# Feed-forward of a two-layer trunk: the gated products turned by transposing transfers on 16-bit planes in place of TensorE transposes

## The chip, the core and the metric

One core of one Trainium2 chip runs one launch of the kernel. The metric is the device time of a launch in microseconds. A core has these engines, each with an instruction stream of its own that it works through in order: TensorE (PE in the profile: matmuls and transposes, with PEld for its weight loads), VectorE (DVE), ScalarE (ACT), GpSimd (POOL) and SyncE (SP), which here only issues transfers. SBUF is the memory on the chip, PSUM the place where TensorE writes its results, and 16 DMA engines move data between the chip's main memory and SBUF or inside SBUF.

## What is computed

A residual stream `h` of 256 tokens and 1024 features goes through two layers. Each layer is a feed-forward, a token mixer and another feed-forward; the mixer is a gated recurrence in the first layer and attention in the second. So there are four feed-forwards, and the change touches nothing else:

```python
def swiglu(x, w_gate, w_up, w_down):
    return (jax.nn.silu(x @ w_gate) * (x @ w_up)) @ w_down

f = swiglu(rms_norm(h, ffn1_pre_g[layer]), ffn1_w_gate[layer], ffn1_w_up[layer], ffn1_w_down[layer])
h = h + 0.5 * rms_norm(f, ffn1_post_g[layer])
```

`w_gate` and `w_up` have 1024 x 2816 elements, `w_down` 2816 x 1024. All data are 32-bit floats.

## The kernel before

**Tiles.** The 256 tokens are two tiles of 128, called t = 0 and t = 1. A matrix product is made to 32-bit accuracy from three matmuls on operands that are split into an upper part (rounded, name ending in hi) and a lower part (what is left, ending in lo): `mm3`, lines 181 to 185, whose three matmuls are lines 183, 184 and 185.

**Weights.** A weight unit is 128 x 1024 elements, 512 KB. `load_raw` (lines 156 to 165) has SP issue its transfer into one of `RAW` = 5 buffers `raw`; `split` (lines 167 to 179) makes the upper part `whi` on ACT (line 173) and the lower part `wlo` on DVE (line 177), each in a ring of `WB` = 9 buffers.

**Order of the work.** `items` is a list of pairs of a preparation (load and split of a unit) and a piece of work for one t. `run` (lines 376 to 389) sets the order on PE by hand: t = 0 goes ahead of t = 1 by `lag` units, which starts at `LAG` = 7 (3 in the first feed-forward), falls to `MID` = 4 within a few units and stays there until the last units. One call of `slot` (lines 367 to 374) is the work of one t on one unit, in a feed-forward 6 matmuls of 512 columns; it ends with a `tick` (lines 84 to 96). `defer(n, f)` has `f` called n + 1 ticks later, counting the tick that ends the same slot. Instructions of PE stay in the order in which they are written; on the other engines a scheduler may move them, and their order is fixed when the program is built.

**A feed-forward** (`ffn_items`, lines 484 to 555) has 44 units of gate and up and 22 of down: five times four units of gate and four of up, 512 columns wide, then four units with gate and up side by side, 256 columns each (`pair_items`). After a gate block, line 498 makes `sil` (ACT). After an up block, `post_up` (lines 502 to 531) multiplies into `prod` (line 510, DVE, 128 tokens x 512 columns). The down product needs these with the columns on the partitions, so they have to be turned. Line 515 has SP copy `prod` into `prr`, a buffer that is typed for TensorE's fast transposes; with `HT` = 5 ticks in between, `hidden_T` (lines 522 to 530) makes four 128 x 128 transposes on PE (line 525; two for the narrow block), for the 512-wide blocks of both t one behind the other, so eight. ACT (line 529) makes the upper part `hhi` from PSUM, DVE (line 530) the lower part `hlo`. A feed-forward has 12 such blocks, six of each t; the whole kernel has 40 wide ones and 8 narrow ones, 176 transposes.

**Buffers around the change.** `prod` has two buffers. The wide `prr` takes the tag `t1` of `hpool` (two buffers, used by the norm steps at the ends of a feed-forward too), the narrow one the tag `sil` (two buffers).

**GpSimd** does little: small steps of the norms (lines 198 and 200), zeroing of gate weights and issue of some small transfers in the first feed-forward, and bias rows of the attention (lines 948 to 975) in the third.

Of the kernel before, what the change touches and what calls it, by code (L numbers as in the profile page):

```python
# [9 lines left out]
F32 = mybir.dt.float32  # L10
F32R = mybir.dt.float32r
BF16 = mybir.dt.bfloat16
AF = mybir.ActivationFunctionType
ALU = mybir.AluOpType
AX = mybir.AxisListType

P = 128
# [9 lines left out]
EPS = 1e-6  # L27
RAW = 5
WB = 9
HT = 5  # L30
LAG = 7
MID = 4
NEG = -1e30
# [10 lines left out]
def trunk_kernel(ctx: ExitStack, tc: tile.TileContext, A: dict, out: bass.AP):  # L44
    nc = tc.nc
# [5 lines left out]
    hpool = ctx.enter_context(tc.tile_pool(name="h", bufs=1))  # L51
# [6 lines left out]
    def nm(s):  # L58
        uid[0] += 1
        return f"{s}_{uid[0]}"  # L60
# [7 lines left out]
    def trbank():  # L68
        return psum.tile([P, 512], F32, tag="tr", name=nm("tr"), bufs=2)
# [11 lines left out]
    def defer(n, fn):  # L81
        pend.append([n, fn])
# [23 lines left out]
    h = [hpool.tile([P, D], F32, tag=f"h{t}", name=f"h{t}") for t in range(2)]  # L106
# [9 lines left out]
    identr = cpool.tile([P, P], F32R, name="identr")  # L116
# [3 lines left out]
    warm = cpool.tile([P, 1], F32, name="warm")  # L120
    nc.scalar.activation(warm, mhalf, AF.Silu)

    def keep_busy(n):

        ps = trbank()
        for _ in range(n):
            nc.tensor.matmul(ps, nc.const_aps.tensor(1.0, (P, P), BF16), nc.const_aps.tensor(1.0, (P, 512), BF16),
                             start=True, stop=True)
# [38 lines left out]
    def split(rawv, parts, n, pieces=1, pin=False):  # L167
# [4 lines left out]
        for c in range(0, n, m):  # L172
            up = nc.scalar.activation(hi[:parts, c:c + m], rawv[:, c:c + m], AF.Copy)  # L173
            if settled[0] or pin:
# [28 lines left out]
    def square_sum(src, acc, f=1.0):  # L203
        junk = spool.tile([P, D], BF16, tag="junk", name=nm("junk"), bufs=1)
        nc.scalar.activation(junk[:, :src.shape[1]], src, AF.Square, scale=f, accum_out=acc)  # L205

# [10 lines left out]
    def x_upper(tp, dest, n):  # L217
# [4 lines left out]
        nc.vector.tensor_tensor(xg, tp.rearrange("p (a b) -> p a b", a=4), g, ALU.mult)  # L222
        nc.scalar.activation(xh[:, 4 * n:4 * n + 4, :], xg, AF.Copy)
        return xg
# [12 lines left out]
    def to_x_tiles(tps, dest):  # L237
# [3 lines left out]
        def operands(k):  # L241
            return tps[k // 4][:, k % 4 * P:(k % 4 + 1) * P], gT[:, gi + k:gi + k + 1]
        with tc.high_priority():
            for k in range(8):
                src, g = operands(k)
                nc.scalar.activation(xh[:, k, :], src, AF.Copy, scale=g)
            for k in range(8):
# [81 lines left out]
    def gain_bcast(src):  # L329
        gb = hpool.tile([P, D], F32, tag="gb", name=nm("gb"), bufs=1)  # L330
        nc.sync.dma_start(gb, src.partition_broadcast(P))
        return gb
# [58 lines left out]
    def proj_items(w, c0, nn, get_x, post, nk=8):  # L391

        kper = min(1024 // nn, 4)
        acc = {}

        for k0 in range(0, nk, kper):
            kn = min(kper, nk - k0)

            def fetch(k0=k0, kn=kn, pieces=1):
                return load_raw(w[k0 * P:(k0 + kn) * P, c0:c0 + nn].rearrange("(k p) n -> p k n", p=P), P, kn * nn, pieces)  # L400

            def prep(fetch=fetch, kn=kn):
                return split(fetch(), P, kn * nn)

            def work(t, u, k0=k0, kn=kn, i=len(items)):
                if i < OPEN:
                    if k0 + kn == nk:
                        post(t, first_acc[t][:, :nn])
                    return
                if k0 == 0:  # L410
                    acc[t] = mmbank()
                ps = acc[t][:, :nn]
                for j in range(kn):
                    k = k0 + j
                    mm3(ps, *get_x(t, k), u.hi[:, j * nn:(j + 1) * nn], u.lo[:, j * nn:(j + 1) * nn], k == 0, k == nk - 1)
                if k0 + kn == nk:
                    post(t, acc[t][:, :nn])
            if len(items) < OPEN:
                first_loads.append(fetch)
            items.append((prep, work))  # L420

    def pair_items(wa, wb, c0, nn, get_x, post):

        acc = {}

        for k0 in range(0, 8, 2):
            def prep(k0=k0):
                raw = new_raw()
                v = raw.rearrange("p (k s n) -> p k s n", k=2, s=2)
                for s, w in enumerate((wa, wb)):  # L430
                    nc.sync.dma_start(v[:, :, s, :], w[k0 * P:(k0 + 2) * P, c0:c0 + nn].rearrange("(k p) n -> p k n", p=P))
                return split(raw, P, 1024)

            def work(t, u, k0=k0):
                if k0 == 0:
                    acc[t] = mmbank()
                for j in range(2):
                    k = k0 + j
                    mm3(acc[t], *get_x(t, k), u.hi[:, j * 512:(j + 1) * 512], u.lo[:, j * 512:(j + 1) * 512], k == 0, k == 7)
                if k0 == 6:  # L440
                    post(t, acc[t][:, :nn], acc[t][:, nn:2 * nn])
            items.append((prep, work))
# [41 lines left out]
    def ffn_items(pool_of, wg, wu, wd, post_g, next_dests, last=False, normed=False):  # L484
        hid = {}
        sil = {}
        box = {}

        def hid_tiles(t):
            if t not in hid:  # L490
                hid[t] = (pool_of().tile([P, 22, P], F32R, tag=f"hhi{t}", name=nm("hhi"), bufs=1),
                          pool_of().tile([P, 22, P], F32R, tag=f"hlo{t}", name=nm("hlo"), bufs=1))
            return hid[t]

        def post_gate(c0, nn):
            def f(t, ps):
                s = pool_of().tile([P, 512], F32, tag="sil", name=nm("sil"), bufs=2)
                nc.scalar.activation(s[:, :nn], ps, AF.Silu, scale=rs[t][:, 0:1])  # L498
                sil[t] = s
            return f  # L500

        def post_up(c0, nn):
            alone = nn < 512
            made = []

            def f(t, ps):
                hh, hl = hid_tiles(t)
                s = sil[t][:, :nn]
                pr = pool_of().tile([P, 512], F32, tag="prod", name=nm("prod"), bufs=2)
                nc.vector.scalar_tensor_tensor(pr[:, :nn], ps, rs[t][:, 0:1], s, ALU.mult, ALU.mult)  # L510
                if alone:
                    moved = pool_of().tile([P, 512], F32R, tag="sil", name=nm("prr"), bufs=2)
                else:
                    moved = hpool.tile([P, 512], F32R, tag="t1", name=nm("prr"), bufs=2)
                nc.sync.dma_start(moved[:, :nn].bitcast(F32), pr[:, :nn])
                made.append((moved, hh, hl))
                if alone or t == 1:
                    todo = list(made)
                    made.clear()
                    defer(HT, lambda: [hidden_T(*m) for m in todo])  # L520

            def hidden_T(moved, hh, hl):
                tp = trbank()
                for j in range(nn // P):
                    nc.tensor.transpose(tp[:, j * P:(j + 1) * P].bitcast(F32R), moved[:, j * P:(j + 1) * P], identr)  # L525
                k0 = c0 // P
                hv = hh[:, k0:k0 + nn // P, :].rearrange("p a b -> p (a b)")
                lv = hl[:, k0:k0 + nn // P, :].rearrange("p a b -> p (a b)")
                nc.scalar.activation(hv, tp[:, :nn], AF.Copy)  # L529
                nc.vector.tensor_tensor(lv, tp[:, :nn], hv.bitcast(F32), ALU.subtract)  # L530
            return f

        i0 = len(items)
        for i in range(5):
            proj_items(wg, i * 512, 512, main_x, post_gate(i * 512, 512))
            proj_items(wu, i * 512, 512, main_x, post_up(i * 512, 512))

        last_up = post_up(2560, 256)

        def post_both(t, pg, pu):  # L540
            post_gate(2560, 256)(t, pg)
            last_up(t, pu)

        pair_items(wg, wu, 2560, 256, main_x, post_both)

        def load_gb():
            box["gb"] = gain_bcast(post_g)

        ahead(i0 + 24, load_gb)

        def post_down(t, accs):
            enter(t, next_dests(t), accs, box["gb"], True, last, normed)

        row_items(wd, [P] * 22, lambda t, k: (hid[t][0][:, k, :], hid[t][1][:, k, :]), post_down, 4 if last else 2)
        return i0
# [697 lines left out]
    parts = [[wpool.tile([P, 1024], F32R, tag=s, name=nm(s), bufs=WB) for s in ("whi", "wlo")] for _ in range(OPEN)]  # L1253
# [202 lines left out]
```

## Time and profile before

| | |
|---|---|
| median of 3 runs | 985.26 us (984.47 to 985.72) |
| the profiled execution | 985.32 us |
| its span, first to last instruction | 983.6 us |
| granted TensorE clock | 0.998 |
| busy in the span | PE 99%, PEld 83%, DVE 62%, ACT 54%, POOL 6% |
| chain that ended last | PE 95%, DVE 2%, issue 2%, ACT 1% |

The span is that of one profiled execution, and 1.7 us of its 985.32 us lie outside. "Busy" is the time in which an engine has an instruction under way. The chain is followed back from the last instruction: at each step to what released it, or to the instruction before it on its engine. Where it runs 95% along PE, time that leaves PE's stream shortens the whole, as long as nothing else becomes late.

### The profile page before, as it was taken

What the parts mean: (1) busy time and instruction counts of PE and PEld (TensorE: products, weight loads), DVE (VectorE), ACT (ScalarE), POOL (GpSimd) and SP (SyncE); (2) the same over time, 40 slices, a digit from 0 to 9 for tenths busy, and PEclk for the clock granted to TensorE, in tenths of its full rate; (3) what the DMA queues carried; (4) which work ended last, traced back from release to release, by engine and by line L of the source; (5) the groups of instructions that cost most, each with busy time, mean ns of one, the idle gap of its engine ahead of it and who ended that gap; (6) DMA issues with size and microseconds to landing.
All of it is one profiled execution on the core that took longest, in us unless ns stands there. A gap on an engine that the chain in (4) does not pass through costs nothing.

```text
span 983.6 us, 13267 instructions
## 1 busy us (share of the span) xinstructions
PE 975.0 (99%) x4863; PEld 812.0 (83%) x4863; DVE 610.2 (62%) x849; ACT 528.1 (54%) x749; POOL 59.9 (6%) x110
## 2 busy tenths in 40 slices
PE   9999999999999999999999999999999999999997
PEld 6888888898978888888899888888887788888886
DVE  6756554678997555554677455555487876555542
ACT  7545443568986544443555344444366855444431
POOL 2400000100002000000113000002020010000000
PEclk9999999999999999999999999999999999999999
DMA  8877665465346766665589767667772467666631
GB/s 290 276 256 245 226 212 192 151 201 162 113 129 201 237 212 209 219 206 189 131 178 307 238 211 214 213 216 237 220 252 85 131 204 235 214 212 214 208 114 43
DMA packets 102966, 196.84 MB, mean 200 GB/s; under 512 B 12974, under 2 KB 36886, under 8 KB 102774
## 3 DMA queue, kind: packets, MB, share of 16 engines
q1 hardware_dynamic: 100102, 188.95, 60.8%
q0 software_dynamic: 2192, 6.51, 2.3%
q8 instruction: 38, 0.62, 0.3%
q10 hardware_dynamic: 608, 0.53, 0.2%
q14 instruction: 26, 0.21, 0.1%
HBM read 182.32 MB, written 3.16 MB: 189 GB/s over the span
## 4 chain that ended last, share of the span: by engine, by line
PE 95%; DVE 2%; issue 2%; ACT 1%; DMA 0%; POOL 0%; POOLq 0%; ACTq 0%; DVEq 0%
PE mm L183 28%; PE mm L185 27%; PE mm L184 27%; PE mm L1023 2%; PE gt L761 2%; PE tr L525 1%; PE mm L1291 1%; PE mm L190 1%; PE mm L191 1%; PE mm L192 1%; DVE wlo L177 1%; PE gt L214 1%; ACT pe L1167 0%; DMA h<-in_x_dram 0%; PE mm L1194 0%
## 5 line engine op out<-in xcount | busy, mean ns | idle before, releaser
L177 DVE TENSOR_TENSOR wlo<-raw,whi 128x1024 fp32r<-128x1024 f32 (+5 forms) x329 | 395.8, 1208 | 265.6 <-ACT whi L173 263.5
L173 ACT ACTIVATE whi<-raw 128x1024 fp32r<-128x1024 f32 (+5 forms) x329 | 342.1, 1046 | 316.7 <-PE mm L185 245.7
L183 PE MATMUL mm<-whi,xhi 128*128 128x512 f32 (+1 forms) x768 | 301.1, 392 | 0.0
L185 PE MATMUL mm<-whi,xlo 128*128 128x512 f32 (+1 forms) x768 | 298.1, 388 | 0.3 <-DVE xlo L228 0.3
L184 PE MATMUL mm<-wlo,xhi 128*128 128x512 f32 (+1 forms) x768 | 298.0, 388 | 0.0
L185 PEld LDWEIGHTS mm<-whi,xlo 128*128 128x128 f32 x768 | 144.2, 188 | 30.7 <-DVE xlo L228 0.7
L183 PEld LDWEIGHTS mm<-whi,xhi 128*128 128x128 f32 x768 | 144.2, 188 | 30.1 <-issue 2.0
L184 PEld LDWEIGHTS mm<-wlo,xhi 128*128 128x128 f32 x768 | 144.3, 188 | 28.1 <-DVE wlo L177 0.3
L183 PE MATMUL mm<-whi,hhi 128*128 128x512 f32 x352 | 137.8, 392 | 0.0
L185 PE MATMUL mm<-whi,hlo 128*128 128x512 f32 x352 | 137.1, 389 | 0.0
L184 PE MATMUL mm<-wlo,hhi 128*128 128x512 f32 x352 | 137.0, 389 | 0.0
L185 PEld LDWEIGHTS mm<-whi,hlo 128*128 128x128 f32 x352 | 66.1, 188 | 13.7
L183 PEld LDWEIGHTS mm<-whi,hhi 128*128 128x128 f32 x352 | 66.1, 188 | 13.4
L184 PEld LDWEIGHTS mm<-wlo,hhi 128*128 128x128 f32 x352 | 66.1, 188 | 13.4
L510 DVE SCALAR_TENSOR_TENSOR prod<-mm,rstd,sil 128x512 f32<-128x512 f32 (+1 forms) x48 | 33.9, 706 | 39.4 <-PE mm L185 31.3
L498 ACT ACTIVATE sil<-mm,rstd 128x512 f32<-128x512 f32 (+1 forms) x48 | 31.2, 653 | 43.1 <-PE mm L185 34.8
L198 POOL TENSOR_SCALAR nv<-ss 128x1 f32<-128x1 f32 x22 | 9.7, 441 | 554.0 <-ACT junk L205 554.0
L529 ACT ACTIVATE hhi<-tr 128x512 fp32r<-128x512 f32 (+1 forms) x48 | 24.8, 558 | 13.2 <-PE tr L525 13.2
L205 ACT ACTIVATE junk<-mm 128x512 bf16<-128x512 f32 x24 | 14.3, 595 | 32.7 <-PE mm L185 32.7
L530 DVE TENSOR_TENSOR hlo<-tr,hhi 128x512 fp32r<-128x512 f32 (+1 forms) x48 | 29.2, 641 | 2.6 <-ACT hhi L529 2.6
L272 DVE TENSOR_TENSOR t<-mm,gb 128x512 f32<-128x512 f32 x24 | 16.2, 687 | 23.6 <-ACT junk L205 23.4
L190 PE MATMUL mm<-xhi,whi 128*126 128x256 f32 (+1 forms) x88 | 24.7, 281 | 0.0
(211 smaller groups left out, 918.6 us busy)
## 6 DMA issues: line engine op xcount, KB each, us to landing
raw<-in_ffn_w_down_dram SPq DMA_DIRECT2D x88, 512.0 KB
raw<-in_ffn_w_up_dram SPq DMA_DIRECT2D x80, 512.0 KB
raw<-in_ffn_w_gate_dram SPq DMA_DIRECT2D x78, 512.0 KB
prr<-prod SPq DMA_DIRECT2D x40, 256.0 KB
raw<-in_rg_w_in_dram SPq DMA_DIRECT2D x10, 504.0 KB
raw<-in_rg_w_out_dram SPq DMA_DIRECT2D x10, 504.0 KB
raw<-in_ffn_w_gate_dram SPq DMA_DIRECT2D x19, 256.0 KB
raw<-in_ffn_w_up_dram SPq DMA_DIRECT2D x16, 256.0 KB
```

Source lines behind the costliest of these rows:

```text
L173: up = nc.scalar.activation(hi[:parts, c:c + m], rawv[:, c:c + m], AF.Copy)
L177: nc.vector.tensor_tensor(lo[:parts, c:c + m], rawv[:, c:c + m], hi[:parts, c:c + m].bitcast(F32), ALU.subtract)
L183: nc.tensor.matmul(ps, xh, wh, start=first, stop=False)
L184: nc.tensor.matmul(ps, xh, wl, start=False, stop=False)
L185: nc.tensor.matmul(ps, xl, wh, start=False, stop=last)
L190: nc.tensor.matmul(ps, wh, xh, start=first, stop=False)
L498: nc.scalar.activation(s[:, :nn], ps, AF.Silu, scale=rs[t][:, 0:1])
L510: nc.vector.scalar_tensor_tensor(pr[:, :nn], ps, rs[t][:, 0:1], s, ALU.mult, ALU.mult)
L529: nc.scalar.activation(hv, tp[:, :nn], AF.Copy)
L530: nc.vector.tensor_tensor(lv, tp[:, :nn], hv.bitcast(F32), ALU.subtract)
L761: nc.tensor.matmul(ps[j][:w, g * S:(g + 1) * S], wv[rows, o:o + w], xc[rows, k, :], start=start, stop=stop, skip_group_check=True)
L1023: nc.tensor.matmul(ps[:, j * S:(j + 1) * S], w, x, start=k == 0 and j == 0 and i == 0, stop=k == 7 and i == 2, skip_group_check=True)
```

## The change

The transposes on PE, the copy of line 515 and the two steps that read PSUM go. A 32-bit number is taken as two 16-bit numbers. GpSimd takes the products apart into a plane of lower and a plane of upper halves (`halves`, in the tag `t1`), a transposing transfer on SP's queue turns the two planes, as 128 x 1024 16-bit elements, back into the bytes of `prod`, GpSimd joins the halves again into `halves`, and ACT and DVE make `hhi` and `hlo` from there. Each block of each t goes by itself: the transfer is called one slot behind the product, the join four slots and the two last steps seven slots behind the transfer's call.

```diff
         def post_up(c0, nn):
...
                 nc.vector.scalar_tensor_tensor(pr[:, :nn], ps, rs[t][:, 0:1], s, ALU.mult, ALU.mult)
-                if alone:
-                    moved = pool_of().tile([P, 512], F32R, tag="sil", name=nm("prr"), bufs=2)
-                else:
-                    moved = hpool.tile([P, 512], F32R, tag="t1", name=nm("prr"), bufs=2)
-                nc.sync.dma_start(moved[:, :nn].bitcast(F32), pr[:, :nn])
-                made.append((moved, hh, hl))
-                if alone or t == 1:
-                    todo = list(made)
-                    made.clear()
-                    defer(HT, lambda: [hidden_T(*m) for m in todo])
-
-            def hidden_T(moved, hh, hl):
-                tp = trbank()
-                for j in range(nn // P):
-                    nc.tensor.transpose(tp[:, j * P:(j + 1) * P].bitcast(F32R), moved[:, j * P:(j + 1) * P], identr)
-                k0 = c0 // P
-                hv = hh[:, k0:k0 + nn // P, :].rearrange("p a b -> p (a b)")
-                lv = hl[:, k0:k0 + nn // P, :].rearrange("p a b -> p (a b)")
-                nc.scalar.activation(hv, tp[:, :nn], AF.Copy)
-                nc.vector.tensor_tensor(lv, tp[:, :nn], hv.bitcast(F32), ALU.subtract)
+                halves = hpool.tile([P, 512], F32, tag="t1", name=nm("pl"), bufs=2).bitcast(U16)[:, :2 * nn]
+                turned = pr.bitcast(U16)[:, :2 * nn].rearrange("p (a b) -> p a b", b=P)
+                nc.gpsimd.tensor_copy(halves.rearrange("p (h f) -> p h f", h=2),
+                                      pr[:, :nn].bitcast(U16).rearrange("p (f h) -> p h f", h=2))
+                defer(1, lambda: hidden_T(halves, turned, hh, hl))
+
+            def hidden_T(halves, turned, hh, hl):
+                m, k0 = nn // P, c0 // P
+                nc.sync.dma_start(turned, halves, transpose=True)
+                hv = hh[:, k0:k0 + m, :].rearrange("p a b -> p (a b)")
+                lv = hl[:, k0:k0 + m, :].rearrange("p a b -> p (a b)")
+
+                def join():
+                    nc.gpsimd.tensor_copy(halves.rearrange("p (f h) -> p h f", h=2),
+                                          turned.rearrange("p (h a) b -> p h (a b)", h=2))
+
+                def parts():
+                    x = halves.bitcast(F32)
+                    nc.scalar.activation(hv, x, AF.Copy)
+                    nc.vector.tensor_tensor(lv, x, hv.bitcast(F32), ALU.subtract)
+                defer(3, join)
+                defer(6, parts)
             return f
```

More of the change, by code (lines that the diff above doesn't have):

```diff
@@ L12 @@
 BF16 = mybir.dt.bfloat16
+U16 = mybir.dt.uint16
 AF = mybir.ActivationFunctionType
@@ L29 @@
 WB = 9
-HT = 5
 LAG = 7
@@ L502, in post_up @@
         def post_up(c0, nn):
-            alone = nn < 512
-            made = []
             def f(t, ps):
```

## The prediction, made before the changed kernel had run

> **What bounds the kernel now.** I read the page from the top: shares of busy time, then the chain that ended last, then the groups.
>
> ```profile
> PE 975.0 (99%) x4863; PEld 812.0 (83%) x4863; DVE 610.2 (62%) x849; ACT 528.1 (54%) x749; POOL 59.9 (6%) x110
> ...
> q1 hardware_dynamic: 100102, 188.95, 60.8%
> ...
> q10 hardware_dynamic: 608, 0.53, 0.2%
> ...
> PE 95%; DVE 2%; issue 2%; ACT 1%; DMA 0%; POOL 0%; POOLq 0%; ACTq 0%; DVEq 0%
> ...
> L525 PE MATMUL tr<-identr,prr 128*128 128x128 f32 x176 | 18.3, 242 | 0.5 <-DVE hlo L530 0.5
> ```
>
> The chain is 95% PE, so PE's stream of instructions sets the end, and the 176 transposes of line 525 stand in it. A matmul's "busy" overlaps the next one's, so their price is not 18.3 us but must be read from the starts. The timeline round one group in the fourth feed-forward, and round one narrow group in the first:
>
> ```profile
> 870.85 0.39 PE L184 MATMUL mm<-wlo,xhi 128*128 128x512 f32 x1
> 871.08 0.39 PE L185 MATMUL mm<-whi,xlo 128*128 128x512 f32 x1
> ...
> 871.31 0.79 PE L525 MATMUL tr<-identr,prr 128*128 128x128 f32 x8
> ...
> 871.94 0.47 PE L183 MATMUL mm<-whi,xhi 128*128 128x512 f32 x1
> ...
> 872.48 0.39 PE L185 MATMUL mm<-whi,xlo 128*128 128x512 f32 x1
> ...
> 142.99 0.40 PE L185 MATMUL mm<-whi,hlo 128*128 128x512 f32 x1
> ...
> 143.88 0.39 PE L185 MATMUL mm<-whi,hlo 128*128 128x512 f32 x1
> ```
>
> Undisturbed matmuls start 0.23 us apart (870.85 to 871.08; 2.72 / 12 = 0.227 by the ACT rows further down, which follow PE unit by unit). A slot of 6 takes 1.36 us, a unit (both t) 2.72, and the spacing of up blocks, one of either t per four units, 10.9 us.
>
> How far the other engines run ahead decides whether PE can use the time. The upper parts of the weights in the second feed-forward, and the waits of SP's queue:
>
> ```profile
> 416.39 1.06 ACT L173 ACTIVATE whi<-raw 128x1024 fp32r<-128x1024 f32 x1 [1.66 <-PE mm L185]
> 419.11 1.06 ACT L173 ACTIVATE whi<-raw 128x1024 fp32r<-128x1024 f32 x1 [1.66 <-PE mm L185]
> 421.83 1.06 ACT L173 ACTIVATE whi<-raw 128x1024 fp32r<-128x1024 f32 x1 [1.66 <-PE mm L185]
> ...
> SPq L161 <- DVE wlo L177: 306.4, 146, 11.3
> ...
> SPq L515 <- DVE prod L510: 68.3, 44, 5.2
> ```
>
> ACT waits for PE every 2.72 us: the ring of nine weight buffers is full. When t = 1 frees unit b, unit b + 9 is made, while t = 0, four units ahead, works on b + 5: four to five units, 11 to 13.6 us, less the split's own 2.3 us. So weights lie ready about 10 us before PE needs them, through all feed-forwards but the start of the first. A late ACT, DVE or SP costs nothing until that lead is used up. SP has a lead of its own on top: it waits for buffers, not for main memory.
>
> **The change part by part.**
>
> *Removed from PE.* Wide group: line 185 at 871.08 to the third matmul behind the transposes at 872.48 is 1.40 us for three pitches of 0.227, so 0.72 extra. Narrow: 142.99 to 143.88 is 0.89, less 0.68: 0.21. There are 20 wide groups (40 blocks, two and two) and 8 narrow ones: 14.4 + 1.7 = 16.1 us. One narrow group stood longer:
>
> ```profile
> 663.53 0.39 PE L185 MATMUL mm<-whi,xlo 128*128 128x512 f32 x1
> 664.46 0.37 PE L525 MATMUL tr<-identr,prr 128*128 128x128 f32 x2 [0.54 <-DVE hlo L530]
> ...
> 665.19 0.40 PE L185 MATMUL mm<-whi,hlo 128*128 128x512 f32 x1
> ```
>
> It waited for DVE to read a PSUM bank out: 1.66 - 0.68 = 0.98 us, so 0.8 more than the others. Nothing takes a transpose bank now, so it goes too: **16.9 us in all**.
>
> *Moved on ACT and DVE.* Each keeps 48 instructions of the same sizes, reading SBUF in place of PSUM. No change: `wlo` reads SBUF for 1225 ns per 1024 columns, half of which is 612, and `hlo` takes 686 from PSUM now.
>
> *Added on POOL:* 96 copies, 80 of them of 1024 16-bit elements per partition. The trace has no such copy. The nearest rows:
>
> ```profile
> L177 DVE TENSOR_TENSOR wlo<-raw,whi 128x1024 fp32r<-128x1024 f32 x292 | 356.1, 1225 | 257.3 <-ACT whi L173 255.4 <-DMA gw<-in_rg_w_x_dram 1.4
> L530 DVE TENSOR_TENSOR hlo<-tr,hhi 128x512 fp32r<-128x512 f32 x40 | 25.8, 686 | 2.6 <-ACT hhi L529 2.6
> ...
> L737 POOL MEMSET gw<- 126x1008 f32 x5 | 4.6, 965 | 0.0
> L948 POOL TENSOR_SCALAR_AFFINE_SELECT bp<-bp 128x512 f32<-128x512 f32 x4 | 2.9, 732 | 20.6 <-DMA bp<-crows 20.6
> L941 POOL TENSOR_SCALAR_AFFINE_SELECT triu<-triu 128x128 f32<-128x128 f32 x1 | 1.0, 957 | 0.1
> masks.py:199 POOL TENSOR_SCALAR_AFFINE_SELECT ident<-ident 128x128 f32<-128x128 f32 x1 | 0.3, 292 | 0.0
> ```
>
> Below: 0.97 us, writing 1008 elements (965 ns). The selects give (732 - 292) / 384 = 1.15 ns per element, hence 0.73 + 512 x 1.15 = 1.3 us, which I take, as it reads and writes. Above: line 941's 957 ns for 128 elements, scaled by eight, 7.7 us. At 1.3 us POOL has 2.6 us of work per 10.9 us; its own time costs nothing.
>
> *The transfer.* Before, SP issued a plain 256 KB copy; now a transposing one of the same bytes, in the same place of SP's order, waiting for POOL's copy instead of DVE's product. Queued behind it on SP are the weight loads, 1.3 us later than before plus whatever a transposing issue takes longer. SP's lead covers that. What it takes of the DMA engines is not in the trace. The whole of two block spacings:
>
> ```profile
> 383.00:405.50 22.50, 22.50 (x106) 18.69 (x105) 12.42 (x12) 10.85 (x13) 0.00 (x0) 1.00 0.67 212
> ```
>
> DMA is 0.67 busy: 7.5 us per block, including the old copy. By the page's queue line a packet takes 0.608 x 983.6 x 16 / 100102 = 96 ns for 1.89 KB, so 256 KB take 0.8 us of the 16 engines. Lower bound: the same 0.8 us. Upper: the built program cuts the transfer into 64 blocks of 16 rows x 128 columns; if each run of 16 turned elements (32 bytes) were a packet at the shortest mean the page gives (q10, 608 packets in 0.2%: 52 ns), 8192 x 52 / 16 = 26.6 us. I take the lower end, as the bytes are the same. Adding 0 to 4 us leaves DMA under 10.9.
>
> *The new wait.* On POOL, split and join of one block stand before the split of the next, and the join waits for the transfer. ACT meets the upper part of a block eight slots, 10.9 us, behind the product; the weights' `whi` are queued behind it, then `wlo`, then PE. The chain: product 0.75 (line 510), split 1.3, transfer, join 1.3, and before either copy up to 1.2 if POOL has to let a DVE instruction end (0.6 on average). For the landing the nearest rows are 256 KB transfers on POOL's queue, issue to landing in the last column:
>
> ```profile
> bias<-crows POOLq DMA_DIRECT2D x4, 256.0 KB, 8.8
> ...
> bp<-crows POOLq DMA_DIRECT2D x4, 256.0 KB, 6.0
> bias1d<-bp POOLq DMA_DIRECT2D x4, 256.0 KB, 5.0
> ...
> L510 DVE SCALAR_TENSOR_TENSOR prod<-mm,rstd,sil 128x512 f32<-128x512 f32 x40 | 30.0, 750 | 32.6 <-PE mm L185 31.3 <-DMA raw<-in_ffn_w_gate_dram 0.7 <-DMA raw<-in_ffn_w_down_dram 0.6
> ```
>
> I take 5.0, the row that reads SBUF; 8.8 is the far end. POOL's cycle L per block is then 0.6 + 1.3 + 5.0 + 0.6 + 1.3 = 8.8 us (far end 1.2 + 1.3 + 8.8 + 1.2 + 1.3 = 13.8), under the spacing of 10.9; with the product 9.6 us, so ACT finds the block ready at 10.9. The buffers are reused two blocks later, 21.8 us. The down product needs the last blocks only some twenty units on. Cost nothing; if that cover goes, see the first rival.
>
> *The ramp.* In the first 45 us ACT waits for weights in place of PE, and POOL issues parameter transfers ahead of its first copy:
>
> ```profile
> 27.30 0.51 POOL L609 DMA_DIRECT2D prow<-in_rg_conv_w_dram  x1 [0.29 <-DMA grow<-in_kv_norm_g_dram]
> ...
> 36.30 0.47 SPq L515 DMA_DIRECT2D prr<-prod  x1
> ...
> 41.24 1.06 ACT L173 ACTIVATE whi<-raw 128x1024 fp32r<-128x1024 f32 x1 [2.77 <-DMA raw<-in_ffn_w_gate_dram]
> ```
>
> The first product is made near 25 us; its copy comes behind those transfers, about 28, and SP's next weight loads some 5 us later than now, where the lead is still growing. It can cost nothing or 5 us; I take 0.5.
>
> *The sum:* 985.32 - 16.9 + 0.5 = **969 us**, against the profiled execution, which stands 0.06 us from the median of 985.26. The lower bound, with no ramp cost and 2 us of smaller stalls gone, is 966.
>
> *What the Trainium skill says against it.* The trace has POOL's small step of line 198 once at 0.70 us and once at 0.23, on the same shape:
>
> ```profile
> 484.99 0.70 POOL L198 TENSOR_SCALAR nv<-ss 128x1 f32<-128x1 f32 x1 [3.11 <-ACT junk L205]
> ...
> 495.89 0.23 POOL L198 TENSOR_SCALAR nv<-ss 128x1 f32<-128x1 f32 x1 [3.04 <-ACT junk L205]
> ```
>
> So something holds POOL up now and then. The Trainium skill, "SBUF — State Buffer", section "Who interferes with whom", has the reason: a DVE instruction with two SBUF inputs and a GpSimd one that reads SBUF exclude each other for the whole instruction, and `wlo` is such an instruction. By that rule the sum stays 969 as long as both fit into 10.9 us; where they don't is the second rival. For the transfer, the Trainium skill, "DMA: Bandwidth & Descriptors", section "Latency and other measured facts", gives 261 GB/s for one kernel's transposes, by which 256 KB would be an estimated 1.0 us in place of 0.8; no run here shows it.
>
> **The rivals.**
>
> *1. The wait on POOL takes the place of the transposes (slower).* Place: POOL's stream, split, wait for landing, join, of one block after the other. If L is over 10.9, each of 11 blocks comes later by L - 10.9, ACT waits for the join, and what is over the lead of about 11 us stops PE: 4 x (11 x (L - 10.9) - 11) us over the four feed-forwards. It decides from L = 12.3, where that is 17 us. At L = 13.8, the far end above, it is 84 us: 1052. For it: the far ends of landing and waits add up to just that, and setting up the transfer's 64 blocks may take SP far longer than the plain copy's 0.47 us. Against: each at its nearest row gives 8.8.
>
> *2. DVE becomes the bound (slower).* If `wlo` and `hlo` cannot run beside POOL's copies, a block needs 4 x 1.225 + 0.69 = 5.6 us of DVE and 2c of POOL, one after the other. 5.6 + 2 x 1.3 = 8.2 fits. With the same lead it decides from c = 3.3 us; at c = 4, 4 x (11 x 2.7 - 11) = 75 us, 1043. Against: the rows of plain POOL work; for it: line 941, scaled.
>
> *3. The transfer crowds out the weights (slower).* DMA needs 7.5 - 0.8 = 6.7 us per block beside it; it decides from 5.6 us per transfer. At the upper bound of 26.6 us the sum would be 4 x (11 x 22.4 - 11) = 940 us more, so that case would give up to about 1900. Against: the same bytes as the copy that PE never waited for.
>
> *4. Part of the gain only.* The ramp, or the narrow blocks at the end of a gate-and-up stretch, where ACT's `sil` of t = 1 stands behind `hhi` of t = 0 and a PSUM bank waits for it without the ring's lead: 1 to 3 us per feed-forward, 972 to 983.
>
> *5. It does not do what it says:* the transfer, being split into many pieces, keeps SP so long that PE waits for weights as before for transposes, and gain and loss cancel: 983.3 to 987.3.
>
> **How the numbers follow.** Forecast (966 to 972) 0.50; rival 4 0.13; rival 5 0.04; rival 1 0.15; rival 2 0.08; rival 3 0.10. Only the first two are faster by over 0.2% (2 us, about what a measurement of this kernel can tell from no change): faster 0.63, same 0.04, slower 0.33. The range goes from 966 to 1040. It holds the forecast, rivals 4 and 5 (0.67) and those halves of rivals 1 and 2 and the fifth of rival 3 that lie below 1040 (0.075 + 0.04 + 0.02), 0.8 in all. The forecast's own range, 966 to 972, is much narrower, as the signs differ.
>
> **What would show it.** Right: no transposes of line 525's kind on PE, matmuls 0.227 us apart through a whole up stretch, POOL's two copies near 1.3 us each, the join 5 us behind the transfer's issue, ACT's `whi` still waiting mostly for PE. Rival 1: ACT waiting in `hhi` for POOL, and POOL waiting for the transfer over 7 us. Rival 2: `wlo` far over 1225 ns, or POOL's copies over 3 us. Rival 3: DMA busy near 100% in the up stretches and ACT waiting for `raw`. Rival 4: gaps on PE at the up-to-down boundaries or before 50 us. What would make the forecast wrong is a transposing transfer that is not like a copy in time, or a POOL copy of 16-bit halves that is not like POOL's 32-bit work.

## The result, and the profile after

The changed kernel takes **995.65 us** (median of 4 runs, 991.57 to 996.49) beside 985.18 us (984.47 to 985.72) for the kernel before on the same chip: ratio 1.0096, 95% interval 1.0082 to 1.0111. It is about 1% slower, where 969.0 was forecast. The profiled execution is the shortest of the four: 991.57 us, a span of 989.9 against 983.6.

The page of the changed kernel: span, busy time, granted clock, the transfers' queue, and the groups of the new instructions (count | busy us, mean ns | idle us before them, and what ended it).

```profile
span 989.9 us, 13061 instructions
...
PE 963.7 (97%) x4687; PEld 800.0 (81%) x4687; DVE 627.9 (63%) x849; ACT 522.1 (53%) x749; POOL 201.7 (20%) x206
...
PEclk9999999999999999999999999997999999999999
...
q1 hardware_dynamic: 139782, 188.96, 64.6%
...
L183 PE MATMUL mm<-whi,hhi 128*128 128x512 f32 x352 | 138.9, 395 | 17.7 <-DVE prod L507 17.7
...
L527 ACT ACTIVATE hhi<-pl 128x512 fp32r<-128x512 f32 (+1 forms) x48 | 28.6, 596 | 178.8 <-POOL pl L522 178.8
L510 POOL COPY pl<-prod 128x1024 uint16<-128x1024 uint16 (+1 forms) x48 | 79.9, 1669 | 204.5 <-DVE prod L507 192.9
L528 DVE TENSOR_TENSOR hlo<-pl,hhi 128x512 fp32r<-128x512 f32 (+1 forms) x48 | 31.0, 646 | 135.5 <-ACT hhi L527 135.5
...
L522 POOL COPY pl<-prod 128x1024 uint16<-128x1024 uint16 (+1 forms) x48 | 63.0, 1313 | 151.8 <-DMA prod<-pl 151.8
```

The 176 transposes are gone from PE (4863 to 4687 instructions). The granted clock has one slice at 7. In the transposes' place PE waits 17.7 us in line 183, the first matmul of a down product, for DVE's `prod`; and ACT and DVE spend 178.8 and 135.5 us waiting in `hhi` and `hlo`. The rows of the kernel before, for comparison:

```profile
L183 PE MATMUL mm<-whi,hhi 128*128 128x512 f32 x352 | 137.8, 392 | 0.0
...
L529 ACT ACTIVATE hhi<-tr 128x512 fp32r<-128x512 f32 (+1 forms) x48 | 24.8, 558 | 13.2 <-PE tr L525 13.2
...
L530 DVE TENSOR_TENSOR hlo<-tr,hhi 128x512 fp32r<-128x512 f32 (+1 forms) x48 | 29.2, 641 | 2.6 <-ACT hhi L529 2.6
```

The wait of line 183 is for a PSUM bank: the up product and the down product take their banks from the same ring of four, `prod` reads one out, and only then may the down product write there. PE's timeline has it at the four boundaries from up to down (last column: idle time before the instruction, and what ended it):

```profile
130.34 0.64 PE L183 MATMUL mm<-whi,hhi 128*128 128x512 f32 x1 [4.96 <-DVE prod L507]
...
142.29 0.50 PE L183 MATMUL mm<-whi,hhi 128*128 128x512 f32 x1 [0.55 <-DVE prod L507]
...
436.61 0.50 PE L183 MATMUL mm<-whi,hhi 128*128 128x512 f32 x1 [1.09 <-DVE prod L507]
...
675.82 0.79 PE L183 MATMUL mm<-whi,hhi 128*128 128x512 f32 x1 [9.26 <-DVE prod L507]
...
929.44 0.50 PE L183 MATMUL mm<-whi,hhi 128*128 128x512 f32 x1 [1.69 <-DVE prod L507]
```

So the gain was made inside the gate-and-up stretches and lost at their ends. To see it, I take the matmuls that both kernels have, in PE's order (all but the transposes), and subtract the start of each in the kernel before from its start in the changed one. The difference falls through each up stretch and jumps at its end (us, negative is ahead; the last row but one is experiment e6 below, which loses nothing):

| | boundary 1, ahead of / behind it | boundary 2 | boundary 3 | boundary 4 |
|---|---|---|---|---|
| start before, us | 113.9 / 142.1 | 432.3 / 459.7 | 647.4 / 676.6 | 921.1 / 948.5 |
| changed kernel | -2.77 / +3.97 | -0.09 / +1.06 | -1.87 / +8.17 | +4.22 / +5.97 |
| e6 | -2.58 / -3.52 | -7.63 / -7.86 | -10.58 / -12.55 | -16.47 / -16.70 |
| lost there, changed against e6 | 7.7 | 1.4 | 12.0 | 2.0 |

The loss is 23.1 us in this execution, the shortest of the four, and 17.7 of them are the waits themselves. Most of the rest is a slower clock behind the long ones. Windows of the changed kernel behind the wait of 9.26 us (us, then busy us and count of PE, PEld, DVE, ACT, POOL, then granted clock, DMA share, GB/s):

```profile
666.00:676.00 10.00, 0.74 (x4) 0.32 (x3) 2.76 (x4) 3.11 (x5) 4.22 (x6) 0.69 0.90 268
676.00:681.00 5.00, 5.00 (x14) 3.96 (x15) 2.60 (x3) 1.66 (x3) 2.62 (x3) 0.59 0.52 123
681.00:686.00 5.00, 5.00 (x24) 4.14 (x23) 2.23 (x3) 2.13 (x2) 2.16 (x3) 1.00 0.87 276
```

In the first 5 us after the wait 14 matmuls start, in the next 5 us 24: ten matmuls of 0.21 us, 2.1 us, are lost to a clock of 0.59.

**Where the lateness comes from.** The timeline of one block in the second feed-forward of the changed kernel, all engines but PE:

```profile
380.18 0.74 DVE L507 SCALAR_TENSOR_TENSOR prod<-mm,rstd,sil 128x512 f32<-128x512 f32 x1
...
380.84 1.21 DVE L177 TENSOR_TENSOR wlo<-raw,whi 128x1024 fp32r<-128x1024 f32 x1
381.06 1.90 POOL L510 COPY pl<-prod 128x1024 uint16<-128x1024 uint16 x1 [3.66 <-DVE prod L507]
...
382.99 1.24 SPq L517 DMA_TRANSPOSE prod<-pl  x1
...
386.19 1.34 POOL L522 COPY pl<-prod 128x1024 uint16<-128x1024 uint16 x1 [3.23 <-DMA prod<-pl]
387.56 0.63 ACT L527 ACTIVATE hhi<-pl 128x512 fp32r<-128x512 f32 x1 [4.67 <-POOL pl L522]
388.10 1.99 ACT L173 ACTIVATE whi<-raw 128x1024 fp32r<-128x1024 f32 x2
388.23 0.69 DVE L528 TENSOR_TENSOR hlo<-pl,hhi 128x512 fp32r<-128x512 f32 x1 [4.08 <-ACT hhi L527]
389.18 2.36 DVE L177 TENSOR_TENSOR wlo<-raw,whi 128x1024 fp32r<-128x1024 f32 x2 [0.26 <-ACT whi L173]
...
391.45 0.74 DVE L507 SCALAR_TENSOR_TENSOR prod<-mm,rstd,sil 128x512 f32<-128x512 f32 x1
...
401.85 0.74 DVE L507 SCALAR_TENSOR_TENSOR prod<-mm,rstd,sil 128x512 f32<-128x512 f32 x1
```

This is a closed loop: product, split, transfer, join, `hhi`, then `whi` behind it on ACT, `wlo`, and the next product behind that on DVE: 380.18 to 391.45, 11.27 us; the next one takes 10.40. Two blocks take 21.7 us against PE's 21.76. There is no slack in it, so a product that is late once, by the ramp or by one slow transfer, stays late. In the first feed-forward the second product starts 4.0 us behind its last matmul, and the tenth, just ahead of the boundary, 7.6 us; in e6 below the second starts 3.8 us behind and the tenth 0.3. Inside the up stretch that costs nothing, as PE goes on into another bank. At the boundary PE needs the bank back.

### The profile page after: what moved, and what is told of

Same layout as the page of the kernel before. It is cut to its first block, busy times and chain, and to the rows that moved or that the text cites. A ratio compares the mean times of both kernels' runs of the same rounds, so it can differ in the third digit from the quotient of the medians.

```text
span 989.9 us, 13061 instructions
## 1 busy us (share of the span) xinstructions
PE 963.7 (97%) x4687; PEld 800.0 (81%) x4687; DVE 627.9 (63%) x849; ACT 522.1 (53%) x749; POOL 201.7 (20%) x206
## 5 line engine op out<-in xcount | busy, mean ns | idle before, releaser
L177 DVE TENSOR_TENSOR wlo<-raw,whi 128x1024 fp32r<-128x1024 f32 (+5 forms) x329 | 414.0, 1272 | 159.1 <-ACT whi L173 156.1
L173 ACT ACTIVATE whi<-raw 128x1024 fp32r<-128x1024 f32 (+5 forms) x329 | 338.0, 1042 | 201.1 <-PE mm L185 137.9
L183 PE MATMUL mm<-whi,hhi 128*128 128x512 f32 x352 | 138.9, 395 | 17.7 <-DVE prod L507 17.7
L527 ACT ACTIVATE hhi<-pl 128x512 fp32r<-128x512 f32 (+1 forms) x48 | 28.6, 596 | 178.8 <-POOL pl L522 178.8
L510 POOL COPY pl<-prod 128x1024 uint16<-128x1024 uint16 (+1 forms) x48 | 79.9, 1669 | 204.5 <-DVE prod L507 192.9
L528 DVE TENSOR_TENSOR hlo<-pl,hhi 128x512 fp32r<-128x512 f32 (+1 forms) x48 | 31.0, 646 | 135.5 <-ACT hhi L527 135.5
L522 POOL COPY pl<-prod 128x1024 uint16<-128x1024 uint16 (+1 forms) x48 | 63.0, 1313 | 151.8 <-DMA prod<-pl 151.8
```

The source lines that it names most:

```text
L177: nc.vector.tensor_tensor(lo[:parts, c:c + m], rawv[:, c:c + m], hi[:parts, c:c + m].bitcast(F32), ALU.subtract)
L183: nc.tensor.matmul(ps, xh, wh, start=first, stop=False)
L510: nc.gpsimd.tensor_copy(halves.rearrange("p (h f) -> p h f", h=2), pr[:, :nn].bitcast(U16).rearrange("p (f h) -> p h f", h=2))
L522: nc.gpsimd.tensor_copy(halves.rearrange("p (f h) -> p h f", h=2), turned.rearrange("p (h a) b -> p h (a b)", h=2))
L527: nc.scalar.activation(hv, x, AF.Copy)
L528: nc.vector.tensor_tensor(lv, x, hv.bitcast(F32), ALU.subtract)
```

## The experiments

The theories as the expectations name them. **A**: this loop, closed by the place at which `hhi` and `hlo` stand in the built order of ACT and DVE, makes all of the loss. **B**: the boundary itself does, with its narrow blocks and the transfers beside them. **C**: GpSimd's copies and DVE exclude each other, which slows DVE. **D**, formed after e1, e3 and e4: two causes, the loop and one displaced transfer. All ratios are to the kernel before, run on the same chip.

### e1: `hhi` and `hlo` held at their place

The delay in `defer(6, parts)` doesn't fix the place: the scheduler put `hhi` one to three weight splits behind its product, and `hlo` two to four. Held in program order, `hlo` stands four to seven weight splits behind it.

```diff
-                    nc.scalar.activation(hv, x, AF.Copy)
-                    nc.vector.tensor_tensor(lv, x, hv.bitcast(F32), ALU.subtract)
+                    tc.keep_in_program_order(nc.scalar.activation(hv, x, AF.Copy))
+                    tc.keep_in_program_order(nc.vector.tensor_tensor(lv, x, hv.bitcast(F32), ALU.subtract))
```

> Changed kernel with hhi (L527) and hlo (L528) held at the place in the order that the six slots ask for, so that four to seven weight splits stand between a product and its hlo on VectorE instead of two or three; copies, transfers and their sizes are as they were. Theory A (the loop product, split, transfer, join, hhi, hlo, weight split, next product takes 10.4 to 11.3 us against TensorE's 10.9 because of where hhi and hlo stand): the waits of hhi and hlo shrink from 8.5 and 7.9 us to under 4, products start within 1 us of their matmuls, TensorE's stalls on PSUM (17.7 us) fall below 3 us, 967 to 973 us. Theory B (the stall belongs to the up-to-down boundary itself, with its narrow blocks and the transfers beside them): products inside a feed-forward may be on time, but the four stalls stay at 10 us or more in sum, 980 to 990 us. Theory C (the GpSimd copies slow VectorE by the shared port): as the changed kernel, 985 to 996 us.

Measured: **975.28 us** (972.94 to 975.72), ratio 0.9882 (0.9866 to 0.9899). The waits of e1 (engine, line, what it waited for: us in total, times, longest):

```profile
ACT hhi L527 <- POOL pl L522: 10.0, 5, 5.5
...
PE mm L183 <- DVE prod L507: 4.5, 1, 4.5
```

The wait in `hhi` went from 178.8 to 10.0 us, three of the four boundaries are clear, and the kernel beats both others. One wait of 4.5 us stays, at the third boundary, so neither A's 967 to 973 nor B's four stalls is quite right; C's 985 to 996 is missed too, with the copies all there. GpSimd's timeline of e1 shows what is special about the third boundary:

```profile
646.25 1.14 POOL L952 DMA_DIRECT2D bias1d<-crows  x1
647.31 0.86 POOL L952 DMA_DIRECT2D bp<-crows  x1
659.86 1.31 POOL L522 COPY pl<-prod 128x1024 uint16<-128x1024 uint16 x1 [11.69 <-DMA prod<-pl]
```

SP issued the block's transposing transfer at 646.33, and its join starts 13.5 us later; it ran beside the 1 MB of `bias1d<-crows`. In the changed kernel and in the kernel before that transfer stands in GpSimd's timeline at

```profile
658.66 1.14 POOL L952 DMA_DIRECT2D bias1d<-crows  x1
```

```profile
539.53 1.14 POOL L952 DMA_DIRECT2D bias1d<-crows  x1
```

Its place in GpSimd's order is the same, fixed at the end of the third feed-forward. Before, nothing stood ahead of it and it ran as soon as its data was there, 120 us early. Now the feed-forward's copies stand ahead of it, each waiting for its product or transfer.

### e3: without the two copies

```diff
-                nc.gpsimd.tensor_copy(halves.rearrange("p (h f) -> p h f", h=2), ...)
...
-                nc.sync.dma_start(turned, halves, transpose=True)
+                nc.sync.dma_start(turned, flat, transpose=True)
...
-                defer(3, join)
```

Here `flat` is the product's words and `turned` is `halves`.

> Changed kernel without both GpSimd copies: the transposing transfer goes from the product straight to the joined tile, and hhi and hlo read its words as 32-bit integers; leaves out the taking apart and joining of the 16-bit planes, so the output is another one. Theory A: the loop is about 3.2 us shorter (two copies of 1.0 to 1.9 and 1.3 us), 7 to 8 us against 10.9: no stall, 967 to 971 us. Theory C: the same, since no copy locks the port. Theory B: the boundary stalls stay, 978 to 988 us. If the transposing transfers slow the weights' loads for all (crowding), TensorE would wait for weights, over 975 us.

Measured: **969.86 us**, ratio 0.9832 (0.9818 to 0.9847), as A and C expect; PE's one wait for a product is 1.3 us. So the forecast's gain is to be had with the transposing transfer in place. GpSimd issues `bias1d<-crows` at 531.1 us here, with no copies ahead of it.

### e4 and e7: idle copies in the kernel before

```diff
                 nc.sync.dma_start(moved[:, :nn].bitcast(F32), pr[:, :nn])
+                idle = spool.tile([P, D], BF16, tag="junk", name=nm("idle"), bufs=1).bitcast(U16)[:, :2 * nn]
+                words = pr[:, :nn].bitcast(U16).rearrange("p (f h) -> p h f", h=2)
+                def aside():
+                    nc.gpsimd.tensor_copy(idle.rearrange("p (h f) -> p h f", h=2), words)
+                aside()
+                defer(4, aside)
```

> Kernel before (turning on TensorE) with two GpSimd copies of the split's form added for each block, one right behind the product and one four slots later, into a tile that nobody reads. Theory A: the copies lengthen some weight splits by about 0.8 us each, but no product waits for them for long: 985 to 988 us. Theory C: the shared port alone makes the products late and costs 5 to 12 us, 990 to 997 us.

Measured: **994.31 us**, ratio 1.0084 (1.0066 to 1.0103). This is C's number, and by the number alone C would have been believed. The trace says otherwise: PE never waits for a split for long, but once for a transfer (waits of e4):

```profile
PE tr L533 <- DMA prr<-prod: 6.4, 1, 6.4
```

It is again the third boundary: GpSimd issues `bias1d<-crows` at 660.18 us in e4, SP the plain `prr<-prod` of a narrow block (128 KB) at 664.68, and that transfer lands 8.7 us after its issue. The same subtraction as above gives 8.6 us lost there. e7 takes that collision away and keeps the copies:

```diff
                 defer(30 + h0, lambda v=v: only_earlier(v))
+            defer(42, lambda: key_rows(kv["bias1"][:, :, :P], 0, NH, 0))
...
-            if i == 0:
-                key_rows(kv["bias1"][:, :, :P], 0, NH, 0)
```

> Kernel before with the idle GpSimd copies of e4 and the 1 MB transfer issued ahead of them. Theory D: the copies did harm only by holding that transfer back until it met prr<-prod (8.7 us to its landing), 985 to 988 us. Theory C (the port shared by GpSimd's copies and VectorE costs by itself): 991 to 997 us.

Measured: **986.49 us**, ratio 1.0007 (0.9998 to 1.0017): no difference from the kernel before. C falls as a theory of the port alone. That the two engines hold each other up is real (`wlo` takes 1281 ns on average in e7, 1225 in the kernel before); it costs nothing here, and PE never waits for a weight.

### e5 and e6: the displaced transfer put back

e5 is the changed kernel with e7's edit of the 1 MB transfer; e6 has both that edit and e1's.

> Changed kernel, order of hhi and hlo as it was, with one edit elsewhere: the 1 MB transfer bias1d<-crows (L952), which GpSimd's queue issued at 658.66 us behind the copies of the third feed-forward, is issued ahead of them, right behind the masks that precede it in program order (about 540 us, where the kernel before issued it). Theory D (two causes: that transfer, held back by the copies in GpSimd's in-order queue, meets the transposing transfer at the third boundary and costs 10.0 us of the lag there; the serial loop costs 6.7, 1.2 and 1.8 us at the other three): the stall of 9.3 us at the third boundary falls below 2 us, the other three stay, 979 to 984 us. Theory A alone (the loop makes all of it): the third stall stays over 5 us, 987 to 995 us.

> Both edits together: hhi and hlo held at their place in the order, and the 1 MB transfer ahead of the copies. Theory D: nothing of the loss is left, TensorE's waits on PSUM under 1 us, 968 to 971 us, which is the forecast of 969. If the boundary itself were to blame: the stall of 4.5 us that the order alone left at the third boundary stays, 973 to 976 us.

Measured: e5 **988.62 us** (987.72 to 994.51), ratio 1.0037 (1.0019 to 1.0055); e6 **968.81 us** (968.70 to 969.20), ratio 0.9828 (0.9813 to 0.9842). In e5 the third wait shrinks from 9.26 to 3.77 us, not below 2 as D expected, and the time misses D's 979 to 984. D's two causes are right, its share of them was off: at that boundary, too, the loop's lateness was part of the wait, since e6, which differs from e5 only in the order, has none. Two more things happen there. The edit moves four instructions on each of ACT and DVE at that boundary, and GpSimd's steps for the bias rows stand between the copies. In e5 SP issued a block's transposing transfer at 659.24 us, and its join starts 5.7 us later (median 3.63), right behind a bias step that had waited for a transfer of its own:

```profile
664.33 0.63 POOL L948 TENSOR_SCALAR_AFFINE_SELECT bp<-bp 128x512 f32<-128x512 f32 x1 [3.56 <-DMA bp<-crows]
664.92 1.34 POOL L522 COPY pl<-prod 128x1024 uint16<-128x1024 uint16 x1
```

No run takes these steps away by themselves. The rows of e6: PE on the page, `wlo` in the groups by form, and the wait in `hhi`:

```profile
PE 959.0 (99%) x4687; PEld 797.9 (82%) x4687; DVE 644.6 (67%) x849; ACT 526.7 (54%) x749; POOL 192.2 (20%) x206
```

```profile
L177 DVE TENSOR_TENSOR wlo<-raw,whi 128x1024 fp32r<-128x1024 f32 x292 | 386.8, 1332 | 217.0 <-ACT whi L173 215.2
```

```profile
ACT hhi L527 <- POOL pl L522: 3.5, 4, 1.9
```

PE waits for no product at all. The full 16.7 us are there (table above), while `wlo`, at 1332 ns against the 1225 of the kernel before, is held up as C says: being held up does not make the loss by itself. It may still have a share in the changed kernel's loop: 32 of the 40 wide splits take 1.90 us or more there, against 1.04 for the other eight, and 0.86 us is as much as e8 below takes out of the loop. No run separates this share. In the timeline of e6 the same stretch has no wait left in `hhi`:

```profile
383.09 0.62 ACT L527 ACTIVATE hhi<-pl 128x512 fp32r<-128x512 f32 x1
...
384.35 0.75 DVE L507 SCALAR_TENSOR_TENSOR prod<-mm,rstd,sil 128x512 f32<-128x512 f32 x1
...
393.33 0.75 DVE L507 SCALAR_TENSOR_TENSOR prod<-mm,rstd,sil 128x512 f32<-128x512 f32 x1 [0.35 <-PE mm L185]
```

The second of these products waits for PE, as the products of the kernel before do.

### e8: a plain transfer in place of the transposing one

```diff
-                nc.sync.dma_start(turned, halves, transpose=True)
+                nc.sync.dma_start(turned.rearrange("p a b -> p (a b)"), halves)
```

> The changed kernel with the 1 MB transfer ahead (as e5) and a plain transfer of the same bytes as 16-bit words in place of the transposing one, every engine's order as in e5; leaves out the turning of the hidden tiles. Theory D: the loop is shorter by 1 to 2.5 us and has slack against 10.9 us, the three stalls that e5 keeps fall below 3 us in sum, 968 to 974 us. If the transposing transfer is no dearer than a plain one in this place: as e5, 979 to 984 us.

Measured: **973.86 us** (972.14 to 977.68), ratio 0.9883 (0.9860 to 0.9907), 14.8 us under e5. The order is e5's but for eight positions on DVE and six on ACT, late in the first feed-forward and at the third boundary. (e2, a plain transfer without the early 1 MB transfer, has no time.) SP and GpSimd in e8, to be held against 382.99 and 386.19 above:

```profile
387.01 0.47 SPq L517 DMA_DIRECT2D prod<-pl  x1
```

```profile
389.48 2.37 POOL L522 COPY pl<-prod 128x1024 uint16<-128x1024 uint16 x1 [2.50 <-DMA prod<-pl]
```

From issue to join 2.47 us in place of 3.20, and over all 48 blocks a median of 2.75 in place of 3.63 in e5. Less than 1 us in a loop without slack is the difference between stalls at every boundary and one wait of 3.4 us, at the third. The other three boundaries have none, as D expects. At the third a join stands behind a bias step here too, 6.5 us behind its transfer's issue.

### e9 and e10: which wait closes the loop, and how far back is enough

e9 is e6 with only `hlo` held in order; e10 is e6 with `defer(8, parts)`.

> As e6 (968.8 us), but only hlo (L528, VectorE) is held at its place in the order; hhi (L527, ScalarE) goes back to where the changed kernel has it, one to three weight halves behind the product. The transfer bias1d stays early, as in e5 (988.6 us), whose two engines both have the changed kernel's order. If VectorE's wait in hlo closes the loop (the product is queued behind it): stalls gone, 968 to 972 us. If ScalarE's wait in hhi closes it (whi and sil are queued behind it, and the weight splits and products wait for those): products late again, 978 to 989 us.

> As e6, with both held at eight slots instead of six, as far behind the product as the changed kernel's text was read to put them. Theory D: six slots already left no wait on TensorE, so nothing is to be had, 968 to 970 us. If the tiles are the next bound (two buffers of t1 and of prod are held longer): products wait for GpSimd's join or the split for hlo, TensorE stalls again, over 972 us.

Measured: e9 **990.90 us** (986.28 to 992.75), ratio 1.0045 (1.0027 to 1.0062); e10 **968.64 us** (968.48 to 969.47), ratio 0.9823 (0.9792 to 0.9854). The waits of e9:

```profile
ACT hhi L527 <- POOL pl L522: 185.6, 48, 6.5
...
PE mm L183 <- DVE prod L507: 12.7, 6, 4.2
```

DVE has no wait in `hlo` left, and nothing is won: **ScalarE's wait in `hhi` closes the loop**, by the `whi` queued behind it (DVE now waits 280.1 us for `whi`, against 151.1 in e5). Whether the place of `hlo` matters at all, no run shows. Two slots more than e6 bring nothing, since PE is the bound again; the two buffers of `t1` and `prod` are enough. Of the versions that leave nothing out, e1, e6 and e10 beat both kernels, the last two by the whole gain.

## Why the prediction was wrong, point by point

The time lies inside the stated range of 966 to 1040 by luck: the part above 987 us was held for rivals 1 to 3, and none of them came about as described.

- **16.9 us leave PE:** right. e6 ends 16.7 us ahead of the kernel before, the ramp's 0.3 us included.
- **GpSimd's copies, 1.3 us each:** right, with the 0.6 us allowed for being held up. The split takes 1.04 us alone (394.22 us in e6) and 1.90 when a `wlo` is under way, 1.67 on average in the changed kernel; the join mostly 1.34.
- **The transfer, landing 5.0 us, 0.8 us of the DMA engines:** landing was over-estimated, 3.2 us to the join in the block shown and a median of 3.46 over all 48. The engines' time was under-estimated: the queue is busy 0.646 x 989.9 - 0.608 x 983.6 = 41.5 us longer, 0.86 us more for each of 48 transfers, in 39,680 more packets. That cost nothing, and rival 3 did not come about.
- **GpSimd's cycle of 8.8 us:** on the safe side; 381.06 to the end of the join at 387.53 is 6.5 us. So rival 1 had the right wait (ACT in `hhi`, for the join) with the wrong loop and the wrong price: what repeats every block is not GpSimd's cycle but the longer way through ACT and DVE to the next product, and it decides from PE's 10.9 us, not from 12.3.
- **"ACT meets the upper part of a block eight slots, 10.9 us, behind the product": this step failed.** The number was read from the ticks in the text, but ticks only say when an instruction is written; on ACT and DVE the scheduler decides. In the block shown ACT came to `hhi` at 382.89 us, 2.7 us behind the product's start, and over all blocks it waits there 178.8 us. With the place held (e6, e10) the forecast comes true: 968.8 and 968.6 against 969.0.
- **"Cost nothing" with the weights' lead of about 10 us as the cover:** the cover was the wrong one. PE never ran out of weights. What a late product holds up is its PSUM bank, and at the boundary there is no lead in that. Rival 4 named the place and the chain: at the third boundary ACT makes `hhi` at 674.46, the narrow `sil` behind it at 674.79, and the product that frees the bank starts at 675.28. Its price was 1 to 3 us per feed-forward; it cost 7.7, 1.4, 12.0 and 2.0.
- **Not in the sum at all:** a transfer on GpSimd's queue that the new copies delay. The copies were priced as time of GpSimd; that each of them makes what is queued behind it wait for its product was not. In the kernel before with idle copies this alone costs the 0.8% between e4 and e7.
- **The ramp, 0.5 us:** right in e6, whose matmuls at 29 us are 0.34 us behind those of the kernel before. In both, the first feed-forward's products start late (4.0 and 3.8 us for the second one); only e6 makes it good.
- **Rival 2, the port that GpSimd and DVE share:** the rule of the Trainium skill, "SBUF — State Buffer", "Who interferes with whom", agrees with the trace (a split of 1.90 us against 1.04, `wlo` 1332 against 1225 ns). In e6 and e7 (0.07%) it left the sum alone, as forecast; in the changed kernel its 0.86 us stand in the loop without slack, and their share is not shown.

How the loss divides between the two causes follows from the four versions with and without each edit. Against the kernel before on the same chip, the changed kernel is at +10.5 us, e5 (transfer early) at +2.4, e1 (order held) at -10.8 and e6 (both) at -17.4. So the order alone costs 19.8 us, the late transfer alone 6.6, and both together 27.9: to within 1.5 us they add up, and the changed kernel's four executions lie 4.9 us apart. What stays open is the share of the port within the loop, and that of the bias steps at the third boundary.

## What to carry to other kernels

Before a wait is called covered, follow it round until it comes back to its own start, through every in-order queue it passes, and take the positions from the built order, not from the text; a loop as long as the bottleneck's own period loses nothing by itself, but never makes up for a delay. Then ask which resource the late step gives back (here a PSUM bank, not weights) and where the bottleneck needs it. A new instruction on a quiet queue also delays everything pinned behind it: look for transfers there, and try the cure before believing a theory that fits the time.

## What the runs showed of the hardware

**A long wait of PE cost more than its length.** After the waits of 9.3, 6.4, 5.0 and 4.5 us, and after one of 3.4 us in e8, the clock is down: its mean over the next 5 us is 0.50 to 0.66. Windows behind that last wait, which ended at 661.06 us, and then, of the changed kernel, behind its wait of 1.09 us that ended at 436.61:

```profile
661.00:666.00 5.00, 4.94 (x15) 3.90 (x16) 2.37 (x3) 1.32 (x2) 3.01 (x3) 0.66 0.73 186
666.00:671.00 5.00, 5.00 (x24) 4.12 (x23) 2.42 (x3) 2.28 (x3) 2.21 (x3) 1.00 0.81 280
```

```profile
438.00:443.00 5.00, 5.00 (x24) 4.14 (x23) 1.65 (x2) 2.05 (x3) 0.92 (x2) 1.00 0.82 285
```

The short wait leaves the clock at 1.00. The Trainium skill, "TensorE: Matmul & The Clock Gate", "Part 1: The HAM clock gate (the "warmup" mystery)", says that the array falls to half rate after an idle window of about 3.4 us and comes back after a busy one; the windows agree, with 0.59 and 0.66 as means over 5 us. No run here kept PE busy through such a wait, so that the clock's share, some 2 us a time, is read from the windows alone.

**A small transfer beside 1 MB on another queue took about three to four times as long:** 8.6 us to its join in the changed kernel (658.74 to 667.29 us) and 13.5 in e1, for 256 KB that take 3.2 undisturbed; and 8.7 us to its landing for a plain one of 128 KB in e4, where 256 KB take 2.5 us to the join in e8.
